# The price table of a kernel's own scheduler is replaced

## The chip, the cores and the metric

The kernel runs on one core of a Trainium2 chip. The metric is device time in microseconds (us) of one execution; the number quoted for a kernel is the median over its runs. The program is a whole two-block transformer step in fp32, and its inputs are read from HBM once per execution.

## The reference

A first block of two layers works on 512 latent tokens and 256 context tokens of width 1024. Each layer modulates its input (`w_ada`), projects it (`w_in`), runs four mixers of 256 columns each, gates the result, projects it out (`w_out`) and normalises:

```python
h = x * (1.0 + scale[:, None]) + shift[:, None]
...
o_f, _ = gla_chunk_scan(q, k_f, i, lf_f, s_cf)      # mixer a: gated linear attention, both directions
...
p = jax.nn.softmax(logits, axis=-1)                 # mixer b: dense attention with two key heads
...
w = p[:, :, 0] - lam * p[:, :, 1]                   # mixer c: differential attention
...
lw = jnp.where(allowed[None, :, None, None], lw, -jnp.inf)   # mixer d: window of 128 and all context
```

A second block of one layer works on the 512 latent tokens: a spatial gating unit, a sparse attention, two convolutions, gated branch projections, `w_out_2`, and an MLP of width 4096 with a squared ReLU.

## The kernel before

All big projections are done as three TensorE matmuls on rounded halves: a weight tile `raw` is loaded by a DMA, rounded to `whi` (fp32r), and the remainder goes to `wlo` (`split`, line 537); activations stand as such pairs too (`h`, `yh`/`yl`, `mix`, `hid`). `mm3` issues hi by hi, hi by lo, lo by hi. Everything else on TensorE is plain fp32 or fp32r: the scores of the attention mixers (`kc`, `kb` against `qs`), transposes against `ident`, and the products with V, which are written PV below (`vc`, `bdv`, `v` against the probabilities `p`).

What order the program's instructions stand in is set while the kernel is built, by a scheduler in the kernel itself. Every stage is a Python generator that yields the tiles it needs next. There are two kinds. **Fillers** are the weight stages, taken in a fixed sequence (`CFG["order"]`, line 2473; `choose`, line 679, lets the next one begin when SBUF has room for it). **Acts** are the stages of the mixers: attention units (`seg_c` line 1227 for mixer c, `seg_bd` line 1356 for b and d), the level chain of mixer a (`j_a`, line 1494), and small follow-ups. At most `wc`, `wb`, `wd` = 4 units of a segment run at a time, one more when no filler is left.

`turn` (line 649) picks what is emitted next. It holds an estimate of the time at which each engine is free and each tile is ready (`Est`, line 211). An act whose tiles are ready by the estimated PE time goes first; if none is, the filler goes; if that is not ready either, the estimated PE time jumps to the first that will be. `Est.op` (line 247) adds an instruction: it starts when its engine is free and its inputs are ready, and its output is ready `LAG` after its end. The prices of the instructions are in `K.time` (line 550). Two other decisions read the same estimates: `best` (line 481) sends a copy, a scaling or a subtraction that is marked `"*"` to the engine that would end it first, and `Psum.pick` (line 428) chooses the bank that is free first.

One unit of mixer c for a latent query tile does this: two score products per head pair into 768 columns of `banks`; on DVE a row maximum (`sm`); on ACT an exponential with a row sum (`p`); reciprocals; a scaling of one `p`; on DVE a `scalar_tensor_tensor` that combines the two; six transposes on PE; a copy back into `p`; and, once both heads of a tile are there, 12 PV matmuls of 128 columns (6 key tiles, 2 heads). Mixer a runs, per pair of heads, one product of `ks` and `qs` and then seven levels in a chain: a copy to `ks`, 12 matmuls of `qh` with `ks` in the first layer and 8 in the second (`level_mm`, line 1477), a masked copy into `att`, and updates of `qh` and `kh`.

At the start of the program the first `h` tiles are made by `co_first_h` (line 955): a scaled activation on ACT, then `split` into the pair.

The build runs twice with the same decisions: once to collect the lifetimes of the SBUF tiles, once to emit. All instructions pass through `Eng` (line 282 in the profile's rows).

Of the kernel before, what the change touches and what calls it, by code (L numbers as in the profile page):

```python
# [11 lines left out]
F32R = mybir.dt.float32r  # L12
# [6 lines left out]
D, S, CL = 1024, 512, 256  # L19
# [191 lines left out]
class Est:  # L211


    LAG = 90.0

    def __init__(self):
        self.t = dict(P=0.0, A=0.0, V=0.0, G=0.0, D=0.0)
# [29 lines left out]
    def op(self, eng, cost, outs, ins, lag=None):  # L247
        start = self.t[eng]
        for ap in ins:
            w, r, i = self.touch(ap)  # L250
            start = max(start, w[i].max())
        for ap in outs:
            w, r, i = self.touch(ap)
            start = max(start, w[i].max() - (self.LAG if eng != "D" else 0.0), r[i].max())
        end = start + cost
        self.t[eng] = end
        lag = self.LAG if lag is None else lag
        for ap in ins:
            w, r, i = self.touch(ap)
            r[i] = np.maximum(r[i], end)  # L260
        for ap in outs:
            w, r, i = self.touch(ap)
            w[i] = end + lag


class Eng:
# [5 lines left out]
    def __getattr__(self, op):  # L272
        f = getattr(self.real, op)

        def call(*a, **kw):
            aps = [x for x in a if hasattr(x, "ap") and hasattr(x, "tensor")]
            outs, ins = aps[:1], aps[1:]
            for n, x in kw.items():
                if hasattr(x, "ap") and hasattr(x, "tensor"):
                    (outs if n in ("accum_out", "out") else ins).append(x)  # L280
            self.k.time(self.eng, op, outs, ins, kw)
            return f(*a, **kw)  # L282
        return call
# [174 lines left out]
class K:  # L458
# [91 lines left out]
    def time(self, eng, op, outs, ins, kw):  # L550
        est = self.est
        if op == "dma_start":
            est.t["D"] = max(est.t["D"], est.t["P"])
            o = outs[0]
            n = int(np.prod(o.shape)) * 4
            est.op("D", 30.0 + n / 360.0, outs, ins, 2000.0)
            return
        if op in ("add_instruction",):
            return
        o = outs[0]  # L560
        n = int(np.prod(o.shape[1:]))
        if eng == "P":
            if op == "transpose":
                c = 107.0
            else:
                k = ins[0]
                m = int(np.prod(k.shape[1:]))
                if k.dtype == F32R:
                    c = max(107.0, n / 2.4)
                else:  # L570
                    c = max(107.0 if m > 64 else 67.0, n * (0.417 if m > 64 else 0.22 if m > 32 else 0.11)) * (2 if n < 512 and m > 64 else 4 if m > 64 else 2)
                    c = max(214.0, n * 1.67) if m > 64 else max(135.0, n * 0.89) if m > 32 else max(60.0, n * 0.42)
                    if k.shape[0] == 64:
                        c /= 2
            est.op("P", c, outs, ins)
            return
        for a in ins:
            n = max(n, int(np.prod(a.shape[1:])) if len(a.shape) > 1 else 1)
        if eng == "A":
            c = 60.0 + 0.95 * n + (90.0 if "accum_out" in kw else 0.0)  # L580
        elif eng == "V":
            ps = any(a.tensor.name == self.bank_name for a in outs + ins)
            fast = op in ("tensor_copy", "tensor_scalar", "memset") and not ps
            c = 70.0 + (0.6 if fast else 1.1) * n
        else:
            c = 90.0 + (2.0 if op == "tensor_tensor" else 1.0) * n
            if kw.get("op") == ALU.pow:
                c = 500.0 + 165.0 * n
        est.op(eng, c, outs, ins)

    @property
# [1934 lines left out]
```

## Time and profile before

| | |
|---|---|
| time, median of 3 runs | 1966.51 us (1965.34 to 1966.84) |
| profiled execution: time, span | 1970.03 us, 1968.3 us |
| granted TensorE clock, mean | 0.976 |
| PE busy | 1856.5 us, 94% |
| DVE, ACT, POOL busy | 1204.4, 622.7, 522.9 us |
| HBM read | 152.12 MB |

PE's busy time is the time in which at least one matmul is under way; what is left of the span is idle time, and a lowered clock makes busy time longer. In the trace the names of buffers stand without their numbers. A plain fp32 matmul that is no transpose stands in the trace as two records; an fp32r matmul or a transpose as one.

### The profile page before, as it was taken

What the parts mean: (1) busy time and instruction counts of PE and PEld (TensorE: products, weight loads), DVE (VectorE), ACT (ScalarE), POOL (GpSimd) and SP (SyncE); (2) the same over time, 40 slices, a digit from 0 to 9 for tenths busy, and PEclk for the clock granted to TensorE, in tenths of its full rate; (3) what the DMA queues carried; (4) which work ended last, traced back from release to release, by engine and by line L of the source; (5) the groups of instructions that cost most, each with busy time, mean ns of one, the idle gap of its engine ahead of it and who ended that gap; (6) DMA issues with size and microseconds to landing.
All of it is one profiled execution on the core that took longest, in us unless ns stands there. A gap on an engine that the chain in (4) does not pass through costs nothing.

```text
span 1968.3 us, 28571 instructions
## 1 busy us (share of the span) xinstructions
PE 1856.5 (94%) x11446; PEld 1539.2 (78%) x11446; DVE 1204.4 (61%) x2055; ACT 622.7 (32%) x1275; POOL 522.9 (27%) x453
## 2 busy tenths in 40 slices
PE   6899999899999999899998899999999999999999
PEld 4688667798877788786886787878788778888887
DVE  2648775655657747766566969764533665545542
ACT  2335444345520145444444321243423211000100
POOL 1314333532222324543233454411211220000000
PEclk9999989999999899999999999999999999999999
DMA  9100321100233301002124322121223222332121
GB/s 359 54 22 23 130 76 59 60 23 33 76 99 126 102 12 44 22 22 97 55 75 142 103 84 73 60 71 43 97 75 123 96 86 75 97 129 86 66 96 63
DMA packets 45380, 159.22 MB, mean 81 GB/s; under 512 B 5040, under 2 KB 5552, under 8 KB 44992
## 3 DMA queue, kind: packets, MB, share of 16 engines
q1 hardware_dynamic: 42224, 148.54, 21.9%
q10 hardware_dynamic: 3024, 8.85, 1.3%
q8 instruction: 90, 1.47, 0.3%
q14 instruction: 42, 0.34, 0.1%
HBM read 152.12 MB, written 5.26 MB: 80 GB/s over the span
## 4 chain that ended last, share of the span: by engine, by line
PE 42%; DVE 12%; POOL 4%; issue 3%; ACT 2%; DMA 1%; ACTq 0%; POOLq 0%; DVEq 0%; SPq 0%
PE banks L282 42%; DVE cacc L282 3%; POOL t L282 2%; DVE t L282 1%; DVE wlo L282 1%; DVE z L282 1%; DVE sm L282 1%; DVE h L282 1%; DVE p L282 1%; ACT p L282 1%; DVE xr L282 0%; DVE whi L282 0%; DVE gt L282 0%; POOL wlo L282 0%; DVE xn L282 0%
## 5 line engine op out<-in xcount | busy, mean ns | idle before, releaser
L282 PE MATMUL banks<-h,whi 128*128 128x512 f32 (+1 forms) x1968 | 584.0, 380 | 5.9 <-ACT h L282 2.8
L282 PEld LDWEIGHTS banks<-h,whi 128*128 128x128 f32 x1968 | 355.4, 192 | 68.2 <-ACT h L282 3.3
L282 PE MATMUL banks<-h,wlo 128*128 128x512 f32 (+1 forms) x984 | 368.6, 375 | 0.0
L282 PE MATMUL banks<-whi,h 128*128 128x256 f32 (+3 forms) x1344 | 337.5, 334 | 14.4 <-DVE h L282 7.9
L282 DVE TENSOR_TENSOR wlo<-raw,whi 128x1024 fp32r<-128x1024 f32 (+2 forms) x175 | 222.9, 1277 | 104.5 <-PE banks L282 59.7
L282 PEld LDWEIGHTS banks<-whi,h 128*128 128x128 f32 x1344 | 237.5, 195 | 40.4 <-DVE h L282 9.4
L282 PE MATMUL banks<-wlo,h 128*128 128x256 f32 (+3 forms) x672 | 221.8, 331 | 6.9 <-DVE wlo L282 5.6
L282 POOL TENSOR_TENSOR wlo<-raw,whi 128x1024 fp32r<-128x1024 f32 (+2 forms) x41 | 103.4, 2525 | 464.5 <-DMA out<-z 299.8
L282 PEld LDWEIGHTS banks<-h,wlo 128*128 128x128 f32 x984 | 188.0, 191 | 32.8 <-DVE wlo L282 0.4
L282 DVE TENSOR_REDUCE sm<-banks 128x1 f32<-128x768 f32 (+5 forms) x192 | 140.0, 750 | 59.7 <-PE banks L282 57.0
L282 ACT ACTIVATE p<-banks,sm 128x768 f32<-128x768 f32 (+5 forms) x192 | 141.3, 739 | 91.3 <-DVE sm L282 83.3
L282 ACT CAST whi<-raw 128x1024 fp32r<-128x1024 f32 (+2 forms) x88 | 88.3, 1006 | 224.0 <-PE banks L282 152.1
L282 PE MATMUL banks<-whi,hid 128*128 128x512 f32 x512 | 157.9, 389 | 0.0
L282 PEld LDWEIGHTS banks<-wlo,h 128*128 128x128 f32 x672 | 131.1, 195 | 18.1 <-DVE wlo L282 7.4
L282 DVE CAST whi<-raw 128x1024 fp32r<-128x1024 f32 (+2 forms) x104 | 74.9, 724 | 114.7 <-PE banks L282 97.1
L282 PEld LDWEIGHTS banks<-whi,hid 128*128 128x128 f32 x512 | 96.1, 188 | 20.0
L282 PE MATMUL banks<-ident,p 128*128 128x128 f32 x656 | 98.0, 282 | 10.2 <-DVE att L282 2.3
L282 ACT COPY p<-banks 128x768 f32<-128x768 f32 (+5 forms) x118 | 74.0, 633 | 92.9 <-PE banks L282 90.7
L282 PE MATMUL banks<-wlo,hid 128*128 128x512 f32 x256 | 99.6, 389 | 0.0
L282 POOL TENSOR_TENSOR t<-t,mhalf 128x1 f32<-128x1 f32 (+5 forms) x51 | 64.1, 1260 | 132.0 <-DVE t L282 128.4
L282 PEld LDWEIGHTS banks<-ident,p 128*128 128x128 f32 x656 | 75.4, 143 | 30.4 <-issue 7.6
L282 ACT ACTIVATE rl<-banks 128x512 f32<-128x512 f32 (+1 forms) x35 | 19.7, 562 | 169.2 <-PE banks L282 169.2
(334 smaller groups left out, 2963.3 us busy)
## 6 DMA issues: line engine op xcount, KB each, us to landing
raw<-wm SPq DMA_DIRECT2D x64, 512.0 KB, 3.5
raw<-win SPq DMA_DIRECT2D x60, 512.0 KB, 3.7
raw<-wada SPq DMA_DIRECT2D x48, 512.0 KB, 3.9
raw<-wgate SPq DMA_DIRECT2D x32, 512.0 KB, 3.5
raw<-wout SPq DMA_DIRECT2D x24, 512.0 KB, 3.5
raw<-w2f SPq DMA_DIRECT2D x10, 512.0 KB, 3.4
xr<-xtok SPq DMA_DIRECT2D x6, 512.0 KB, 4.6
x<-z SPq DMA_DIRECT2D x6, 512.0 KB, 2.6
```

What stands on the lines that cost most here:

```text
L282: return f(*a, **kw)
```

## The change

The prices in `K.time` and the readiness lags in `Est` are set to other numbers. No stage, tile, window or filler sequence is edited; the order of the instructions and the engines that `best` picks follow from the new numbers. In `Est.op`, `LAG` for DVE, ACT and POOL goes from 90 to 50 ns; PE's own lag, 90 before, is now 200. On PE the plain fp32 products get a price by the columns of the stationary operand (`m`) and its rows.

```diff
--- before.py
+++ after.py
@@ -211,7 +211,7 @@
 class Est:
 
 
-    LAG = 90.0
+    LAG = 50.0
 
     def __init__(self):
         self.t = dict(P=0.0, A=0.0, V=0.0, G=0.0, D=0.0)
@@ -251,7 +251,7 @@
             start = max(start, w[i].max())
         for ap in outs:
             w, r, i = self.touch(ap)
-            start = max(start, w[i].max() - (self.LAG if eng != "D" else 0.0), r[i].max())
+            start = max(start, w[i].max() - (0.0 if eng == "D" else 200.0 if eng == "P" else self.LAG), r[i].max())
         end = start + cost
         self.t[eng] = end
         lag = self.LAG if lag is None else lag
@@ -560,32 +560,32 @@
         o = outs[0]
         n = int(np.prod(o.shape[1:]))
         if eng == "P":
+            k = ins[0]
+            m = int(np.prod(k.shape[1:]))
             if op == "transpose":
-                c = 107.0
+                c = 110.0
+            elif k.dtype == F32R:
+                c = max(108.0, 0.4475 * n)
+            elif m > 64:
+                c = 0.42 * n if k.shape[0] == 64 else max(120.0, 1.74 * n)
+            elif m > 32:
+                c = 140.0 if k.shape[0] == 64 else max(54.0, 0.42 * n)
             else:
-                k = ins[0]
-                m = int(np.prod(k.shape[1:]))
-                if k.dtype == F32R:
-                    c = max(107.0, n / 2.4)
-                else:
-                    c = max(107.0 if m > 64 else 67.0, n * (0.417 if m > 64 else 0.22 if m > 32 else 0.11)) * (2 if n < 512 and m > 64 else 4 if m > 64 else 2)
-                    c = max(214.0, n * 1.67) if m > 64 else max(135.0, n * 0.89) if m > 32 else max(60.0, n * 0.42)
-                    if k.shape[0] == 64:
-                        c /= 2
-            est.op("P", c, outs, ins)
+                c = 0.213 * n
+            est.op("P", c, outs, ins, 200.0)
             return
         for a in ins:
             n = max(n, int(np.prod(a.shape[1:])) if len(a.shape) > 1 else 1)
         if eng == "A":
-            c = 60.0 + 0.95 * n + (90.0 if "accum_out" in kw else 0.0)
+            c = 170.0 + 0.93 * n + (100.0 if "accum_out" in kw else 0.0)
         elif eng == "V":
             ps = any(a.tensor.name == self.bank_name for a in outs + ins)
             fast = op in ("tensor_copy", "tensor_scalar", "memset") and not ps
-            c = 70.0 + (0.6 if fast else 1.1) * n
+            c = 110.0 + 0.58 * n if fast else 125.0 + 1.1 * n + (70.0 if op in ("scalar_tensor_tensor", "copy_predicated") else 0.0)
         else:
-            c = 90.0 + (2.0 if op == "tensor_tensor" else 1.0) * n
+            c = 200.0 + (2.3 if op == "tensor_tensor" else 1.05) * n
             if kw.get("op") == ALU.pow:
-                c = 500.0 + 165.0 * n
+                c = 700.0 + 165.0 * n
         est.op(eng, c, outs, ins)
 
     @property
```

**PE, mixer a's first pair of heads in the first layer.** `qh,ks` are the level matmuls, `kc,qs` scores of mixer c, `whi` and `wlo` with `h` the fillers. Before, levels 3 and 4 (`ks_2082`, `ks_2135`):

```order
L282 MATMUL banks<-qh_1805,ks_2082 128x128 x12
L282 MATMUL banks<-kc_1478,qs_1996 128x512
L282 MATMUL banks<-kc_1478,qs_1996 128x256
L282 MATMUL banks<-qh_1805,ks_2135 128x128 x3
L282 MATMUL banks<-kc_1478,qs_1996 128x512
L282 MATMUL banks<-kc_1478,qs_1996 128x256
L282 MATMUL banks<-qh_1805,ks_2135 128x128 x5
L282 MATMUL banks<-kc_1478,qs_1996 128x512
L282 MATMUL banks<-kc_1478,qs_1996 128x256
L282 MATMUL banks<-qh_1805,ks_2135 128x128 x4
L282 MATMUL banks<-ident_69,p_2028 128x128 x6
```

The same pair after, level 4 (`ks_2063`) and what follows it up to level 5:

```order
L282 MATMUL banks<-qh_1767,ks_2063 128x128 x12
L282 MATMUL banks<-kc_1557,qs_2024 128x512
L282 MATMUL banks<-kc_1557,qs_2024 128x256
L282 MATMUL banks<-kc_1557,qs_2024 128x512
L282 MATMUL banks<-kc_1557,qs_2024 128x256
L282 MATMUL banks<-ident_69,stg_2032 128x128 x4
L282 MATMUL banks<-whi_1608,h_95 128x256
L282 MATMUL banks<-wlo_1609,h_95 128x256
L282 MATMUL banks<-whi_1608,h_96 128x256
L282 MATMUL banks<-whi_1608,h_95 128x256
L282 MATMUL banks<-wlo_1609,h_95 128x256
L282 MATMUL banks<-whi_1608,h_96 128x256
```

And after, the start of that pair: the product with `qs`, levels 0 and 1.

```order
L282 MATMUL banks<-qs_1393,ks_1770 128x128 x12
L282 MATMUL banks<-kc_1557,qs_1733 128x512
L282 MATMUL banks<-kc_1557,qs_1733 128x256
L282 MATMUL banks<-qh_1767,ks_1820 128x128 x12
L282 MATMUL banks<-kc_1557,qs_1733 128x512
L282 MATMUL banks<-kc_1557,qs_1733 128x256
L282 MATMUL banks<-kc_1557,qs_1741 128x512
L282 MATMUL banks<-kc_1557,qs_1741 128x256
L282 MATMUL banks<-qh_1767,ks_1851 128x128 x2
L282 MATMUL banks<-kc_1557,qs_1741 128x512
L282 MATMUL banks<-kc_1557,qs_1741 128x256
L282 MATMUL banks<-qh_1767,ks_1851 128x128 x10
```

In the program before, levels 3 and 4 have only scores between them, and between the other levels of the pair stand fillers. In the new one, filler rows follow level 4, and the places with nothing but scores between level products are the two at the pair's start.

**PE, the end of the second layer's attention.** `kb,qs` and `dmask` are scores of mixer d, `ident,p` its transposes, `p,bdv` its PV matmuls, `yh`, `yl` with `whi`, `wlo` the output projection, which is the filler there. Before, the last scores and what follows:

```order
L282 MATMUL banks<-dmask_76,identr_74 128x128
L282 MATMUL banks<-kb_8746,qs_9405 128x256 x4
L282 MATMUL banks<-dmask_76,identr_74 128x128
L282 MATMUL banks<-kb_8746,qs_9405 128x256
L282 MATMUL banks<-whi_9425,yh_8919 128x512
L282 MATMUL banks<-ident_69,p_9358 128x128 x5
L282 MATMUL banks<-wlo_9426,yh_8919 128x512
L282 MATMUL banks<-whi_9425,yl_8920 128x512
L282 MATMUL banks<-whi_9425,yh_9011 128x512
L282 MATMUL banks<-wlo_9426,yh_9011 128x512
L282 MATMUL banks<-whi_9425,yl_9012 128x512
```

After, the last scores and what follows:

```order
L282 MATMUL banks<-kb_8746,qs_9494 128x256 x3
L282 MATMUL banks<-dmask_76,identr_74 128x128
L282 MATMUL banks<-kb_8746,qs_9494 128x256 x4
L282 MATMUL banks<-dmask_76,identr_74 128x128
L282 MATMUL banks<-kb_8746,qs_9494 128x256
L282 MATMUL banks<-ident_69,p_9467 128x128 x5
L282 MATMUL banks<-p_9467,bdv_7969 64x128
L282 MATMUL banks<-ident_69,p_9489 128x128 x5
L282 MATMUL banks<-whi_9155,yh_8834 128x512
L282 MATMUL banks<-ident_69,p_9509 128x128 x4
L282 MATMUL banks<-p_9489,bdv_7969 64x128
```

Before, 18 rows of the output projection stand between those scores and the transposes of the last units; the piece shows the first six of them and the transposes of an older unit. After, one projection row stands between the last scores and the transposes of the unit that they belong to (`p_9509`), beside transposes and a PV matmul of the two units ahead of it.

**DVE, the first `h` tiles.** `x_17` and `x_18` are columns of the input, `h_95` and `h_96` the pair for the latent tokens, `h_98` the remainder for the context tokens.

```order
 L282 CAST h_95<-x_17_99 128x512
 L282 TENSOR_TENSOR h_96<-x_17_99,h_95 128x512
+L282 CAST h_95<-x_18_101 128x512
 L282 TENSOR_TENSOR h_98<-x_17_99,h_97 128x256
 L282 TENSOR_TENSOR h_96<-x_18_101,h_95 128x512
-L282 TENSOR_TENSOR h_98<-x_18_101,h_97 128x256
 L282 TENSOR_TENSOR mod_103<-banks,vec_61 128x4
```

The rounding of every second `h` tile, which stood on ACT, is now on DVE ahead of the remainder of the tile before it, and one remainder has left DVE. The same swap follows in the next round and in the last. Over the whole program DVE has 166 subtractions into `wlo` where it had 175, and POOL 50 where it had 41; of the scalings of `p`, DVE has 30 (43 before), POOL 56 (41), ACT 66 (68). From a point near 1350 us of the old trace to the end, PE's rows are the same but for buffer numbers.

## Rows read from the trace of the kernel before

**Rows 1.** The page: the span.
```profile
span 1968.3 us, 28571 instructions
```

**Rows 2.** Stretches: length, then busy time of PE, PEld, DVE, ACT, POOL; PEclk; DMA share; GB/s.
```profile
114.00:565.00 451.00, 429.25 (x3511) 359.61 (x3510) 297.13 (x589) 216.41 (x478) 146.91 (x135) 0.97 0.18 59
710.00:1079.00 369.00, 343.52 (x2708) 288.04 (x2707) 251.16 (x426) 177.39 (x350) 139.74 (x131) 0.97 0.19 61
1079.00:1300.00 221.00, 199.03 (x1010) 174.42 (x1009) 187.63 (x312) 57.75 (x132) 103.42 (x83) 0.95 0.24 81
```

**Rows 3.** Whom PE waited for: us in total, times, longest us.
```profile
...
PE banks L282 <- DVE att L282: 7.6, 7, 2.4
PE banks L282 <- ACT p L282: 6.8, 14, 1.2
PE banks L282 <- POOL qh L282: 6.3, 3, 3.4
PE banks L282 <- POOL ks L282: 4.1, 3, 2.6
PE banks L282 <- DVE p L282: 3.5, 7, 1.8
PE banks L282 <- DVE qs L282: 3.5, 3, 2.5
PE banks L282 <- ACT qs L282: 2.7, 3, 1.3
```

**Rows 4.** Instructions by form: engine, operation, shapes xcount | busy us, mean ns | idle before.
```profile
L282 DVE TENSOR_REDUCE sm<-banks 128x1 f32<-128x768 f32 x96 | 88.6, 949 | 19.6 <-PE banks L282 17.8 <-ACT p L282 1.1
...
L282 ACT ACTIVATE p<-banks,sm 128x768 f32<-128x768 f32 x96 | 86.3, 904 | 57.3 <-DVE sm L282 49.6 <-POOL bd L282 2.7 <-PE banks L282 2.1
...
L282 ACT ACTIVATION_READ_ACCUMULATOR p<-banks,sm 128x1 f32 x192 | 38.1, 199 | 0.0
...
L282 DVE SCALAR_TENSOR_TENSOR p<-p,sm,p 128x768 f32<-128x768 f32 x32 | 36.8, 1153 | 6.5 <-ACT p L282 4.4 <-POOL p L282 1.9
```

**Rows 5.** PE's timeline from 330 and 386 us: start, us, engine, tile xcount.
```profile
330.70 1.55 PE L282 MATMUL banks<-p,bdv 128*64 128x128 f32 x24
332.18 0.98 PE L282 MATMUL banks<-ident,p 128*128 128x128 f32 x7
...
386.67 1.61 PE L282 MATMUL banks<-qh,ks 64*128 64x128 f32 x24
388.20 0.66 PE L282 MATMUL banks<-p,bdv 128*64 128x128 f32 x8
```

**Rows 6.** A stretch of MLP matmuls of 512 columns alone, columns as in rows 2.
```profile
1700.00:1750.00 50.00, 50.00 (x223) 41.39 (x222) 22.34 (x27) 1.65 (x2) 0.00 (x0) 1.00 0.28 95
```

**Rows 7.** Instructions by form, PE: records of the PV and level matmuls.
```profile
L282 PE MATMUL banks<-p,bdv 128*64 128x128 f32 x736 | 54.0, 283 | 0.3 <-DVE p L282 0.2
...
L282 PE MATMUL banks<-qh,ks 64*128 64x128 f32 x560 | 47.0, 301 | 10.4 <-POOL qh L282 6.3 <-ACT ks L282 1.5 <-DVE sm L282 1.2
...
L282 PE MATMUL banks<-p,vc 128*64 128x128 f32 x416 | 30.7, 278 | 0.2 <-DVE p L282 0.2
...
L282 PE MATMUL banks<-qs,ks 64*128 64x128 f32 x80 | 8.1, 346 | 3.7 <-POOL ks L282 3.7
```

**Rows 8.** The stretch 255 to 271 us, and a row of PE's timeline in it.
```profile
255.00:271.00 16.00, 12.40 (x93) 9.74 (x94) 13.96 (x21) 7.04 (x13) 7.39 (x7) 0.80 0.08 29
...
263.20 0.71 PE L282 MATMUL banks<-qh,ks 64*128 64x128 f32 x6 [2.00 <-POOL qh L282]
```

**Rows 9.** The end of the second layer's attention, columns as in rows 2.
```profile
1064.00:1079.00 15.00, 12.87 (x84) 9.63 (x85) 6.70 (x11) 6.74 (x11) 6.23 (x3) 1.00 0.29 96
```

**Rows 10.** Timelines of DVE and POOL near 35 us and of DVE near 66 us.
```profile
35.08 2.45 DVE L282 CAST h<-x 128x512 fp32r<-128x512 f32 x1 [0.29 <-ACT x L282]
...
34.88 2.37 POOL L282 TENSOR_TENSOR wlo<-raw,whi 128x1024 fp32r<-128x1024 f32 x1 [13.26 <-DMA raw<-wada]
...
65.85 0.43 DVE L282 CAST h<-x 128x512 fp32r<-128x512 f32 x1 [0.89 <-ACT x L282]
```

## Prediction

> **What bounds the kernel now.** I read the span first [rows 1], then the stretches [rows 2], then what ended PE's waits [rows 3]. TensorE carries the time. In the two attention stretches it is busy for 429.25 of 451 us and 343.52 of 369 us, so it idles 21.8 and 25.5 us, 47.3 together. The granted clock there is 0.97 in both: at most 0.03 x 820 = 24.6 us more go to stretches at the lower of its two levels (1.2 against 2.4 GHz), and these follow idle time, as the run at 255 us shows, with 3.6 us idle and a clock of 0.80 [rows 8]. So 71.9 us is all that a better order could take out of attention. In the stretch from 1079 to 1300 us DVE is busy 187.63 of 221 us and PE idles 22.0; that is DVE's work, and an order of stages does not shorten it. From about 1350 us on PE's rows are unchanged, and I price that part at nothing, since no wait there sees another producer in another place.
>
> The waits of attention are of two kinds [rows 3]. Those on the results of units (`p` from ACT 6.8 and DVE 3.5, `qs` from DVE 3.5 and ACT 2.7) are 16.5 us. Those on mixer a's level chain (`att` 7.6, `qh` 6.3, `ks` 4.1) are 18.0 us.
>
> **What the new prices say, against the rows.** Take the chain of a unit of mixer c: row maximum, exponential with row sum, combination. The rows have 949 + 904 + 199 + 1153 = 3205 ns [rows 4]. The old formulas give 915 + 880 + 915 = 2710, with three handoffs of 90 2980. The new ones give 970 + 984 + 1040 = 2994, with handoffs of 200, 50 and 50 3294. So the old table was short of the bare durations by 225 ns even with its handoffs, and the new one is 89 over. A matmul of 512 columns takes 50/223 = 224 ns [rows 6]; the price goes from 213 to 229. So far the table comes closer.
>
> It moves away at the small fp32 products. The 24 records of a PV run are 12 instructions by the code (6 key tiles, 2 heads), and they hold PE from 330.70 to 332.18, 123 ns each [rows 5]; the price goes from 135 to 54. A level of 12 instructions takes 386.67 to 388.20, 128 ns each [rows 5]; the price goes from 107 to 54. The new numbers are those of one record, and an instruction has two. With (736 + 416)/2 = 576 PV instructions and (560 + 80)/2 = 320 level instructions [rows 7] the scheduler's PE falls behind by 576 x 69 + 320 x 74 = 63 us over both layers. It then takes results for not ready that are, and emits filler in their place.
>
> **The change part by part.** *Waits on units.* With handoffs and DVE, ACT and POOL priced near the rows, a unit's next step is emitted later and more filler stands ahead of it. Bounds: nothing, where no filler is to be had, and all 16.5 us. I take two thirds, since the shortfall of 225 ns is gone in the table and some waits are of engines' queues that it still has wrong: 11.0 us, and the clock in proportion, 24.6 x 11.0/47.3 = 5.7. Together -16.7.
>
> *Waits on the level chain.* I cost this at nothing, with bounds of 9 us either way (half of 18.0). The order shows why: the levels that stood with only scores between them, where PE waited 2.00 us for `qh` [rows 8], are now followed by filler, but the pair starts with two places of the same kind. What is late next is `qh` again, one level earlier.
>
> *Ends of the layers.* At the end of the second layer the last scores had 18 projection matmuls of 0.224 us behind them, 4.0 us; now it is one. The last units need 3205 ns and more from scores to transposes [rows 4], and that cover is gone. The old end already idled 2.1 of 15 us [rows 9]. I take +3 per layer, since the first layer's last units stand among the projection's first rows in the same way: +6. Bounds: 0, if the filler spent earlier saved as much there, and +13, twice 42% of 16 us, which is what the bare run lost in idle time and clock (3.6 + 3.2 of 16) [rows 8].
>
> *Start.* Three roundings of `h` move from ACT to DVE, ahead of a remainder that PE waits for: 3 x 0.43 us [rows 10] = 1.3, bounds 0 and 2 x that, for ACT gets to its next activation sooner. I take +1.
>
> *Work moved to POOL.* Nine more remainders `wlo` are on POOL. While POOL ran such a one from 34.88 to 37.25, a DVE rounding that takes 0.43 us elsewhere took 2.45, and ended 0.28 us after it [rows 10]. Each can thus hold DVE up for 2.0 us: 18 us at most, nothing at least. DVE idles a third of both attention stretches, 1 - 548.29/820 [rows 2], and not every `wlo` meets such an operation, so I take +2. The 15 more scalings of `p` on POOL are priced near their length in the new table and have filler over them; should that be gone they are part of the ends above.
>
> The Trainium skill, page "SBUF — State Buffer", section "SBUF: two separate sides", says that DVE and GpSimd share a port pair under an exclusive lock, held for a whole instruction, against DVE operations in a two-port mode or with two SBUF inputs. The trace agrees in the one row cited; by that rule alone the sum would have up to +18 in this place where it has +2, and it speaks against moving work to POOL.
>
> **The sum.** -16.7 + 0 + 6 + 1 + 2 = -7.7 us. The profiled execution took 1970.0 us, 1.7 more than its span, and lies 3.5 above the median of the runs. 1970.0 - 7.7 - 3.5 = **1958.8 us**.
>
> **The rivals.** *Cover only moves (no change).* The scheduler has the same fillers and the same units; what one place gains another lacks. For it: the level chain's two bare places before and two after. Half of the gain on units then remains, -8.4 + 9 = +0.6: 1967.1 us. A run of this kernel tells a difference of about 0.2% (3.9 us) from none.
>
> *Filler spent too early (slower).* The 63 us by which the scheduler's PE lags behind are emitted as filler ahead of need, and the units late in each layer run bare, at 42% loss [rows 8]: 26.6 us in place of the 6 above. -16.7 + 26.6 + 3 = +12.9: 1979.4 us. It decides from (16.7 - 3)/0.42 = 33 us of filler on. For it: the tail of the second layer in the new order. Against it: level 4 of the first pair has filler behind it that it lacked.
>
> *POOL holds DVE.* Every added `wlo` blocks DVE for its length and PE waits for it: +18 in place of +2 gives +8.3, 1974.8 us. Against it: the waits on `wlo` are not among the long ones. [...]
>
> *The table does not do what it says*: this is so for the two fp32 prices, and lies in the second rival.
>
> **How the numbers follow.** 0.43 for the forecast, 0.21 for no change, 0.29 for filler spent early, 0.07 for POOL. So faster by over 0.2% 0.43, within it 0.21, slower 0.36. The order of some 8000 rows is new, and single waits of 1 to 3 us fall anew, which no row prices; that is why the chances lie close. Low end: the gain on units and clock twice as large, other terms +5, -28.4: 1938. High end: filler spent early, and POOL at +9 in place of +2: 1986.
>
> **What would show it.** Right: PE's waits on `p` and `qs` fall to some 6 us from 16.5, the clock of both attention stretches rises above 0.97, waits on `att`, `qh`, `ks` stay near 18, and the last 15 us before the second layer's projection idle some 5 us. Wrong: waits on `p` unchanged, or an attention stretch in which idle time gathers at its end; or DVE roundings and remainders that grow longer beside POOL. The forecast falls if the two attention stretches together, 820 us before, do not get shorter by some 10 us.

## The result, and the profile after

The changed kernel takes 1980.17 us, median of 4 runs (1979.28 to 1987.05); beside it the kernel before took 1966.03. The ratio is 1.0085, 95% interval 1.0062 to 1.0107: **slower** by 0.85%, where the forecast said 1958.8 and faster. The time lies in the stated range, and beside the second rival's 1979.4. The profiled execution has a span 9.3 us longer [rows 1], so the traces hold 9.3 of the 14.1 us between the medians.

The page of the changed kernel:

```profile
span 1977.6 us, 28679 instructions
...
PE 1853.5 (94%) x11446; PEld 1534.3 (78%) x11446; DVE 1178.9 (60%) x2040; ACT 625.0 (32%) x1279; POOL 545.4 (28%) x464
```

PE's busy time is 3.0 us shorter than before, so the loss is idle time. To find it, both traces have to be cut at the same work, not at the same microsecond: I cut each where PE had begun the same number of its 11,446 matmul records (449, 3958, 4578, 6867, 7285 and 8293). The second layer's attention is cut once more, ahead of its last 418 records. Stretches of the kernel before, columns as in [rows 2]:

```profile
710.00:1014.20 304.20, 283.90 (x2291) 241.16 (x2289) 210.11 (x346) 145.07 (x280) 117.20 (x115) 0.97 0.15 49
1014.20:1079.10 64.90, 59.73 (x419) 46.96 (x418) 41.15 (x81) 32.33 (x71) 22.54 (x16) 1.00 0.35 118
```

The changed kernel, first layer's attention, then the two pieces of the second's, then the stretch behind it:

```profile
112.50:576.10 463.60, 433.14 (x3510) 361.12 (x3510) 290.44 (x574) 218.67 (x482) 149.19 (x140) 0.98 0.18 60
...
717.80:1006.50 288.70, 276.51 (x2290) 236.14 (x2289) 203.45 (x348) 146.85 (x283) 120.80 (x110) 0.99 0.17 56
1006.50:1084.60 78.10, 63.54 (x419) 49.79 (x419) 43.41 (x82) 34.17 (x75) 26.83 (x19) 0.93 0.22 77
1084.60:1313.70 229.10, 203.15 (x1009) 177.38 (x1009) 177.50 (x312) 58.38 (x129) 92.97 (x75) 0.93 0.23 78
```

The first layer's attention took 451.1 us between the same records and now takes 463.6: 12.5 longer, with 30.5 us of PE idle where 21.8 were. The body of the second layer's is 15.5 shorter, idle 20.3 to 12.2, clock 0.97 to 0.99. Its end is 13.2 longer: idle 5.2 to 14.6, clock 1.00 to 0.93. The stretch behind it grew by 8.1, and what is left (start, first epilogue, the part from 1300 us) shrank by 9.0. The sum is 9.3.

Whom PE waited for, changed kernel (us, times, longest):

```profile
PE banks L282 <- ACT p L282: 16.3, 21, 3.3
...
PE banks L282 <- POOL wlo L282: 10.0, 9, 2.4
...
PE banks L282 <- ACT qs L282: 8.3, 5, 5.9
...
PE banks L282 <- DVE p L282: 4.1, 2, 2.4
...
PE banks L282 <- POOL ks L282: 2.8, 2, 2.0
PE banks L282 <- POOL qh L282: 2.7, 2, 1.5
...
PE banks L282 <- DVE att L282: 2.4, 5, 0.7
...
PE banks L282 <- DVE qs L282: 1.4, 2, 0.8
```

The waits on units, 16.5 us before [rows 3], are 16.3 + 4.1 + 8.3 + 1.4 = 30.1. Those on mixer a's chain, 18.0, are 7.9. On POOL's remainders `wlo` PE waits 10.0 us; the same row of the kernel before:

```profile
PE banks L282 <- POOL wlo L282: 2.7, 3, 1.3
```

By stretch, in us, from the same rows (`p` and `qs` of ACT and DVE; `att`, `qh` and `ks` of DVE and POOL):

| second number: changed kernel | units | level chain |
|---|---|---|
| first layer's attention | 6.0, 15.2 | 6.5, 6.9 |
| second layer's, body | 7.2, 6.6 | 11.5, 1.1 |
| second layer's, end | 2.2, 8.4 | 0, 0 |

So the gain in the body of the second layer is the chain's, which the forecast had at nothing, and hardly the units'. The rows of the body before:

```profile
PE banks L282 <- DVE att L282: 4.6, 3, 2.4
PE banks L282 <- POOL qh L282: 4.3, 2, 3.4
...
PE banks L282 <- POOL ks L282: 2.6, 1, 2.6
```

After, only this one is left of them there:

```profile
PE banks L282 <- DVE att L282: 1.1, 2, 0.6
```

A row "PE <- ACT `p`" is not always a wait for a result. The longest of the first layer stands before transposes that read no `p`:

```profile
218.61 1.51 PE L282 MATMUL banks<-ident,hq 128*128 128x128 f32 x6 [3.32 <-ACT p L282]
```

In the program the first of them writes columns of `banks` that the exponential it waits for still reads: PE waits for a bank, and which bank a stage gets is `Psum.pick`'s choice by the same estimates. Of the 16.3 us on ACT's `p`, 12.1 stand before matmuls that read no `p`, and the program's rows give this reason for each; in the kernel before, 5.0 of 6.8 stand before such matmuls.

The longest wait of all on units, 5.9 us on `qs` at the end of the second layer, shows a cause that the forecast did not have. The timeline of all engines there, changed kernel (start, us, engine, instruction, idle before and what ended it):

```profile
1042.92 0.59 ACT L282 COPY yo<-banks 128x512 f32<-128x512 f32 x1 [3.80 <-PE banks L282]
...
1043.51 1.05 POOL L282 TENSOR_SCALAR bc<-bc 128x1024 f32<-128x1024 f32 x1 [14.51 <-ACT yo L282]
...
1044.64 3.37 POOL L282 TENSOR_TENSOR xr<-xr,bc 128x1024 f32<-128x1024 f32 x1
1047.97 2.33 POOL L282 TENSOR_TENSOR wlo<-raw,whi 128x1024 fp32r<-128x1024 f32 x1
1048.04 3.34 DVE L282 TENSOR_TENSOR xr<-xr,bc 128x1024 f32<-128x1024 f32 x1 [2.23 <-POOL xr L282]
1050.34 0.37 ACT L282 CAST qs<-banks 128x256 fp32r<-128x256 f32 x1 [6.84 <-POOL wlo L282]
1050.77 1.01 PE L282 MATMUL banks<-kb,qs 128*128 128x256 f32 x3 [5.88 <-ACT qs L282]
...
1053.36 1.22 DVE L282 TENSOR_TENSOR xr<-xr,bc 128x1024 f32<-128x1024 f32 x1
```

ACT copies `qs` out of PSUM, and PE had written it 10 us earlier. It waited for POOL's remainder `wlo<-raw,whi`, with which `qs` has nothing to do. The program's rows say why:

```
732 L282 CAST qs_1048_9324<-banks_58 128x256 [waits Pool_49]
320 L282 TENSOR_TENSOR wlo_1041_9290<-raw_1030_9248,whi_1040_9289 128x1024 [waits DMAHW5_49,DVE_49]
```

`qs_1048` was given the SBUF place of `raw_1030`, and must not write there before the last reader of `raw_1030` is done. That reader stood on POOL behind a `bc` that had waited 14.51 us and an `xr` of 3.37. The profile puts the 14.51 down to ACT's `yo`, which `bc` does not read; by the program's rows it waits, beside earlier work on PE, DVE and ACT, for the DMA that brings it, issued at 1036.12.

Two pieces of that end, around this wait and behind the last scores:

```profile
1042.70:1056.00 13.30, 7.42 (x37) 6.59 (x36) 9.18 (x11) 4.25 (x10) 6.72 (x3) 0.74 0.03 11
...
1072.00:1081.20 9.20, 7.51 (x56) 5.30 (x56) 5.57 (x17) 4.82 (x13) 3.28 (x4) 1.00 0.27 100
```

The first has 5.9 us of idle and a clock of 0.74, worth some 1.9 us more by estimate (7.42 x 0.26): 7.8 of the 13.2. The second is the bare place that the forecast had read; it idles 1.7 us at the full clock.

Places are given out by the kernel itself (`Mem.place`, line 360), from the order of allocations and releases. A released place rests as long as the tiles in use and those at rest stay below a `share` of SBUF; it tries shares from 1.0 down until all fits. By the build's own count the kernel before holds at most 206,336 of 212,800 bytes per partition and is placed at share 0.82; the changed one holds 211,456 and gets 0.72.

### The profile page after: what moved, and what is told of

The parts are those of the page before. It is cut to its first block, busy times and chain, and to the rows that moved or that the text cites. A ratio compares the mean times of both kernels' runs of the same rounds, so it can differ in the third digit from the quotient of the medians.

```text
span 1977.6 us, 28679 instructions
## 1 busy us (share of the span) xinstructions
PE 1853.5 (94%) x11446; PEld 1534.3 (78%) x11446; DVE 1178.9 (60%) x2040; ACT 625.0 (32%) x1279; POOL 545.4 (28%) x464
## 3 DMA queue, kind: packets, MB, share of 16 engines
q1 hardware_dynamic: 42224, 148.54, 21.9%
## 4 chain that ended last, share of the span: by engine, by line
PE 71%; DVE 11%; POOL 6%; issue 4%; DMA 4%; ACT 3%; POOLq 0%; SPq 0%; DVEq 0%; ACTq 0%
PE banks L282 71%; DVE sm L282 2%; POOL t L282 2%; ACT p L282 2%; DVE wlo L282 1%; POOL wlo L282 1%; DVE t L282 1%; DMA x<-xT 1%; DMA raw<-wada 1%; DVE h L282 1%; DMA raw<-win 1%; DVE cacc L282 1%; ACT whi L282 1%; DVE z L282 0%; DVE whi L282 0%
## 5 line engine op out<-in xcount | busy, mean ns | idle before, releaser
L282 DVE TENSOR_TENSOR wlo<-raw,whi 128x1024 fp32r<-128x1024 f32 (+2 forms) x166 | 209.4, 1264 | 124.2 <-PE banks L282 58.7
L282 POOL TENSOR_TENSOR wlo<-raw,whi 128x1024 fp32r<-128x1024 f32 (+2 forms) x50 | 124.3, 2489 | 440.0 <-PE banks L282 324.2
L282 DVE CAST whi<-raw 128x1024 fp32r<-128x1024 f32 (+2 forms) x98 | 68.9, 708 | 102.3 <-DMA raw<-wm 62.8
L282 POOL TENSOR_SCALAR p<-p,sm 128x768 f32<-128x768 f32 (+4 forms) x56 | 51.6, 923 | 150.2 <-DVE sm L282 129.9
```

## The experiments

Three theories at the start. **A**: the second rival, fp32 prices per record make the scheduler's PE late, and filler is spent early. **B**: work moved to POOL holds up DVE. **C**: any small change of a price gives another order, and which wait falls where is chance. Ratios below are to the kernel before, with 95% intervals. One thing to know for all of them: the framework that builds the program may put an instruction ahead of others of its engine; in the kernel before about 4% of PE's rows no longer follow the row that the scheduler emitted ahead of them.

**e1: fp32 prices per instruction, otherwise the change.**

```diff
-                c = 0.42 * n if k.shape[0] == 64 else max(120.0, 1.74 * n)
+                c = 0.87 * n if k.shape[0] == 64 else max(120.0, 1.74 * n)
...
-                c = 140.0 if k.shape[0] == 64 else max(54.0, 0.42 * n)
+                c = 140.0 if k.shape[0] == 64 else max(54.0, 0.87 * n)
```

> The changed kernel with its two fp32 prices set per instruction in place of per record (PV and level matmuls of 128 columns 111 instead of 54). Theory A, filler spent early because these prices are too low: the loss at the ends of both layers goes, the gain in their middle stays, about 1960 us (1955 to 1967). Theory B, work moved to POOL collides with DVE (49 remainders wlo stay on POOL): no change, 1976 to 1984. Theory C, any table of about these numbers gives an order of its own, and which wait falls where is chance: anything from 1962 to 1985, and no ordering by the prices.

1965.78 us, 1.0001 (0.9985 to 1.0018): the loss is gone, as A said; C's bounds hold the time too. The build also gave this kernel another placement (share 0.80), so e1 alone does not tell order from places. The end of the second layer's attention in its trace:

```profile
1011.80:1079.10 67.30, 61.54 (x420) 48.86 (x418) 39.19 (x79) 33.09 (x73) 18.91 (x14) 0.95 0.34 105
```

67.3 us, where the change has 78.1 and the kernel before 64.9. B falls here as what the loss needs: 49 remainders are still on POOL.

**e2: the matmul prices of before, the rest of the change.** The `if eng == "P":` branch of the kernel before is put back; `est.op("P", c, outs, ins, 200.0)` stays.

> The changed kernel with all matmul prices of before, only the prices of ACT, DVE and POOL and the lags are new (46 wlo on POOL). Theory A: PV 135 and levels 107 are near or above their length, so no filler is spent early: about 1960 us (1955 to 1967). Theory B: 1974 to 1984. Theory C: anything from 1962 to 1985.

1994.39 us, 1.0141 (1.0118 to 1.0164). A missed by 27 us, and B's and C's bounds do not hold it either. The build's count is again 211,456 bytes, and the share found only 0.64.

**e3: only the matmul prices and PE's lag of the change, in the kernel before.**

> The kernel of before with only the matmul prices and PE's lag of the change (38 wlo on POOL, 41 before). Theory A: filler spent early without the gain on units: slower than the changed kernel, 1980 to 1995. Theory B: as before, 1962 to 1970. Theory C: anything from 1962 to 1985.

1974.77 us, 1.0044 (1.003 to 1.0059). Slower, but 5 us less than A's low end, and more than B said; C's bounds hold it.

**e4: the kernel before with another lag.**

```diff
-    LAG = 90.0
+    LAG = 92.0
```

> The kernel of before with its lag at 92 ns in place of 90, nothing else; more than half of PE's rows come to stand elsewhere. Theories A and B: as before within 3 us, 1963 to 1969. Theory C: off by 5 us or more to either side, though no price is nearer to or further from the trace.

1961.63 us, 0.9976 (0.9963 to 0.9989). Two nanoseconds of lag are worth 4 us, below A's and B's range and short of C's 5, so part of any such difference is chance.

With the shares beside the times (0.78 for e4, 0.82 for before, 0.80 for e1 and e3, 0.72 for the change, 0.64 for e2) a new theory, **D**: places given on too early make the kernel slow. It is tested by other placements with the same emission, engines and prices. For e5, e7 and e8 the placer starts at the share named, and a tile that found no place goes first in the next try; e6 starts the old placer at 0.64.

```diff
-        for share in np.arange(1.0, 0.5, -0.02):
+        for share in np.arange(0.82, 0.5, -0.02):
...
-            for long in (300, 100, 200, 500, 50):
-                at = self.fit(size, f0, rest, long)
+            self.first = []
+            for _ in range(160):
+                at = self.fit(size, f0, rest, 20)
...
+        order = self.first + [i for i in order if i not in self.first]
...
+                self.first = [i] + [j for j in self.first if j != i]
```

> The changed kernel, same emission by its scheduler, but its SBUF tiles are placed so that a freed place rests as long as in the kernel before (share 0.82; the change itself only found a placement at 0.72). Theory D, the new order keeps more tiles alive at once, freed places are handed out sooner, and instructions wait for the last reader of the tile that stood there: 1964 to 1971 us. Theories A (filler spent early) and B (POOL against DVE): unchanged, 1976 to 1984, since order and engines stay. Theory C, chance of single waits: 1970 to 1985.

1958.37 us, 0.9969 (0.9956 to 0.9981): 21.8 faster than the change, 6 below D's range, and faster than the kernel before. The same `qs_1048` in its program and its trace:

```
732 L282 CAST qs_1048_9324<-banks_58 128x256 [waits PE_49,Activation_49]
```

```profile
1038.10 0.37 ACT L282 CAST qs<-banks 128x256 fp32r<-128x256 f32 x1
1038.53 0.42 PEld L282 LDWEIGHTS banks<-kb,qs 128*128 128x128 f32 x3 [0.26 <-ACT qs L282]
```

With another place it no longer waits for POOL, and PE's 5.88 us became 0.26. A and B said no change here: neither is needed for the loss of the kernel as built. The same four stretches as above in this kernel:

```profile
115.70:570.60 454.90, 427.81 (x3511) 361.13 (x3510) 300.15 (x572) 216.02 (x478) 150.72 (x138) 0.98 0.18 60
711.10:1001.60 290.50, 280.28 (x2290) 238.49 (x2289) 205.28 (x343) 149.54 (x286) 114.00 (x109) 0.98 0.18 56
1001.60:1071.90 70.30, 62.56 (x419) 50.66 (x418) 36.79 (x77) 31.26 (x70) 20.14 (x18) 0.93 0.22 79
1071.90:1293.10 221.20, 200.53 (x1010) 174.76 (x1009) 184.02 (x316) 57.38 (x129) 97.12 (x77) 0.95 0.25 81
```

Against the change, 8.7 us went from the first layer, 7.8 from the second layer's end and 7.9 from the stretch behind it; the gain in the body stayed. The waits on units did not go back: they are 21.9 us, most of them in the row

```profile
PE banks L282 <- ACT p L282: 17.0, 20, 2.9
```

One limit: the emission is the same, but which rows pass others follows from the places. Counted in the two built programs, 313 of PE's 10,000 instructions and 936 of DVE's 2,040 have another successor. "Placement" in e5 to e8 means the places and this together.

> The kernel before, same emission by its scheduler, with its tiles placed at share 0.64 in place of 0.82, as the second experiment had. Theory D: 1980 to 1995 us. Theories A and B: unchanged, 1963 to 1969. Theory C: 1960 to 1975.

1980.12 us (1972.63 to 1981.61), 1.0069 (1.0042 to 1.0095): slower by 14, as D said, and outside the ranges of A, B and C.

> The second experiment's kernel (old matmul prices, new prices elsewhere; 1994 us at share 0.64) with its tiles placed at share 0.82. Theory D: 1965 to 1976 us. Theories A and B: unchanged, 1990 to 1997. Theory C: 1980 to 1997.

2006.28 us, 1.0209 (1.0185 to 1.0234): a miss for all theories, 12 slower where D had said some 24 faster.

> The kernel before with its tiles placed at share 0.90 in place of 0.82, same emission. Theory D: faster, 1955 to 1963 us, unless all places rest long enough already at 0.82. Theories A, B: unchanged, 1963 to 1969. Theory C: 1960 to 1972.

1985.33 us, 1.011 (1.0084 to 1.0136): a miss for all again, 19 slower. So the share is no measure of a placement. What stands is that placement, at the same emission, moved three kernels in four trials by -22, +14, +12 and +19 us: as much as the change did.

To separate order from places I held every instruction to the order of its emission and built that with two placements. In the second a place is given on once the former tile's last reader has ended by the scheduler's own estimate, with a margin where there is room; where nothing fits, the margin goes below zero and in the end is dropped.

```diff
-            return f(*a, **kw)
+            r = f(*a, **kw)
+            if r is not None and hasattr(r, "ins"):
+                self.k.tc.keep_in_program_order(r)
+            return r
```

```diff
+            live = np.where(d < i, f0[d] > i, f0[i] > d)
+            gap = np.where(d < i, a[i] - z[d], a[d] - z[i])
+            for m in tiers:
+                hit = d[live | (gap < m)]
```

Here `a` and `z` are a tile's first and last use by the estimate, and `tiers` are the margins, from 8 us down to -4 and to none. The prices under test feed this estimate too.

> The kernel before, with every instruction held to the order in which its scheduler emitted it (the framework that builds the program otherwise lets about 4% of PE's rows pass others); placement at share 0.82 as before. Nothing more is told by it alone; it is the base for the next three. Since a row whose place is not free yet can no longer be passed, 1975 to 2005 us.

> The changed kernel held to its emission order in the same way, placement at share 0.72 as the change has it. Theory D (waits for the former tenant of a place): slower than the kernel before held to its order by 15 us or more. Theory A (filler spent early, a matter of order alone): slower by 10 to 20 us.

> The kernel before held to its emission order, same rows on every engine as the run before last, but tiles placed by the scheduler's own estimated times: a place is given on only once the former tenant's last reader has ended by the estimate, with a margin of up to 8 us where there is room. Theory D: faster than the same order at share 0.82 by 10 to 30 us. Theories A and B: no change, since order and engines are the same.

> The changed kernel held to its emission order, tiles placed by estimated times in the same way. Theory D: faster than the same order at share 0.72 by 20 to 45 us, and within 8 us of the kernel before placed in that way, so that the price table itself is worth little either way. Theory A: 10 to 20 us slower than the kernel before placed in that way, since the order holds the loss.

| | old placement | placed by estimated times |
|---|---|---|
| kernel before | 2017.33 (e9) | 2015.81 (e11) |
| changed kernel | 2063.92 (e10) | 2035.42 (e12) |

All four are held to their emission; the two of a line have the same instructions in the same order on every engine. The old placement costs the changed order 28.5 us, in D's range, and the order before 1.5, where D had said 10 or more. The two orders stay 19.6 apart, as A said, where D had said 8 at most. On the old placement they are 46.6 apart, more than A's 10 to 20, and e9 itself lies 12 above its range. Of the second layer's attention, body and end of e11, then of e12:

```profile
721.90:1023.10 301.20, 280.10 (x2290) 238.16 (x2289) 213.54 (x347) 145.24 (x286) 119.70 (x117) 0.97 0.15 49
1023.10:1097.80 74.70, 62.58 (x420) 49.28 (x419) 55.65 (x93) 33.64 (x73) 25.76 (x17) 0.91 0.35 119
```

```profile
727.90:1031.20 303.30, 283.50 (x2291) 242.07 (x2291) 208.90 (x344) 145.48 (x283) 121.42 (x110) 0.95 0.14 46
1031.20:1122.60 91.40, 69.34 (x420) 53.36 (x419) 55.05 (x97) 35.90 (x80) 28.90 (x21) 0.84 0.29 106
```

The bodies differ by 2.1 us, the ends by 16.7: 12.1 us of idle against 22.1, clock 0.91 against 0.84. That is the second rival's place, but only in part its shape. PE's waits at e12's end are more on weight tiles than on units:

```profile
PE banks L287 <- ACT whi L287: 6.7, 2, 3.8
PE banks L287 <- ACT p L287: 5.2, 2, 4.8
PE banks L287 <- POOL wlo L287: 4.5, 3, 2.4
PE banks L287 <- POOL p L287: 2.5, 3, 1.5
```

Of the 10 us more idle than in e11, some 6 are on units (`p` and `qs` of all engines, 8.2 against 2.4). The longest of those, 4.8, goes back to DVE, where two `xr` products ahead of the unit's reciprocals took 6.55 us while POOL worked on remainders. The 3.8 on `whi` goes back to a DMA of `bc` that ACT waited for.

Which price makes the difference? **F** is the theory that the longer prices and lags of the other engines do. The next four are held and placed in the way of e11 and e12.

> The changed kernel with its fp32 prices per instruction, held to its emission order, tiles placed by estimated times. Base: 2016 us for the kernel before built in that way, 2035 for the changed one. Theory A (fp32 prices per record spend filler early): 2010 to 2020, with the loss at the end of the second layer gone. Theory F (longer prices and lags of DVE, ACT, POOL and PE move units back): 2030 to 2040. Theory C: anywhere from 2000 to 2045.

1992.77 us: 42.6 faster than e12, 23.0 faster than e11, and below the ranges of all three theories. Its body and end:

```profile
709.40:1002.10 292.70, 278.24 (x2291) 239.41 (x2290) 218.27 (x347) 144.20 (x280) 119.94 (x112) 0.98 0.14 46
1002.10:1082.50 80.40, 61.38 (x419) 48.66 (x418) 49.68 (x99) 35.79 (x79) 22.65 (x17) 0.94 0.33 114
```

In the profiles, 11.0 us of the gain on e12 come from the end, 10.6 from the body and 18.5 from what lies ahead of it.

> The changed kernel with the old matmul prices (new lags and new prices of the other engines), held and placed in the same way. Theory A: 2010 to 2020. Theory F: 2030 to 2045. Theory C: anywhere from 2000 to 2045.

2011.04 us: 24.4 faster than e12. A's range holds, and F's does not: the new prices of the other engines without the new matmul prices are not slower here than the kernel before. As built, the same prices were the slowest (e2, e7).

> The kernel before with only the new matmul prices and PE's lag, held and placed in the same way. Theory A: 2030 to 2045. Theory F: 2010 to 2025. Theory C: anywhere from 2000 to 2045.

2019.55 us, 3.7 over e11: a miss for A and in F's range. The new matmul prices, among the old prices of the other engines, cost next to nothing.

> The kernel before with lag 92 in place of 90, held and placed in the same way. Theories A and F: 2013 to 2019, as the kernel before. Theory C: off by 8 us or more, to either side.

2006.43 us, 9.4 under e11, as C said, and a miss for A and F: orders with prices 2 ns apart differ by this much. The 42.6 and 24.4 are above it, the 3.7 is not. But each table was built once, with a placement of its own, and e10 against e12 shows a placement to be worth 28.5 at one order; so 24.4 is not clear of chance, and 42.6 is one trial.

The last two change both, prices and placement, in the kernel as it is built, where rows may pass others:

> The changed kernel with its fp32 prices per instruction and its tiles placed at share 0.82, built as the change is (rows may pass others). If the two causes add, 1935 to 1950 us (1980 less 14 and less 22). If either alone takes back what there is, 1953 to 1963, as the changed prices with the better placement. If placements fall by chance, 1950 to 1980.

> The same prices, tiles placed by the scheduler's estimated times, rows may pass others. If the two causes add, 1935 to 1950 us. If either alone takes back what there is, 1953 to 1963. If placements fall by chance, 1950 to 1980.

1963.01 us, 0.9983 (0.9972 to 0.9995), and 1966.63 us, 1.0003 (0.9991 to 1.0016). They don't add. The first lies at the edge of "either alone", the second only in the range for chance. The fastest kernel of the study stays e5: the prices of the change as they are, with another placement.

## Why the prediction was wrong

The sum was -7.7 us; medians moved by +14.1, and the two attention stretches, which the forecast wanted some 10 us shorter, are 10.2 longer (820.2 to 830.4). Term by term:

- **Waits on units, -16.7 with the clock: failed.** The step was "I take two thirds, since the shortfall of 225 ns is gone in the table". The waits rose from 16.5 to 30.1 us: in the first layer from 6.0 to 15.2, at the end of the second from 2.2 to 8.4, and in its body they stayed (7.2 to 6.6). Two things were wrong in it. Three quarters of the largest row are waits for a bank and not for a unit's result; the forecast had read the whole row as results, and taken its two thirds of all of it. And I had taken a change of prices for a change of order alone. Order also decides which tiles are alive together, and so who stands on whose place; no term of the sum had that. With other places (e5) the waits are 21.9, still above 16.5: the step fails there too.
- **Level chain, 0: right in the first layer, wrong in the second.** 18.0 to 7.9 us, 1.1 beyond the bound of 9. In the first layer, whose order was read, it stayed (6.5 to 6.9); the fall is the second layer's (11.5 to 1.1), whose level order was not read. It is the one large gain of the change, and the forecast did not count on it.
- **Ends of the layers, +6 (0 to 13): the wrong place.** The second layer's end alone cost 13.2. Behind the last scores, where one projection row stands in place of 18, PE idles 1.7 us; some 7.8 go with the one wait for a place ahead of that, and e5's end is 7.8 shorter.
- **Start, +1: -1.6** (112.5 us to the same record, 114.1 before).
- **POOL, +2: 7.3**, but not in the way foreseen. PE waited for POOL's remainders themselves, 10.0 us against 2.7. DVE's own remainders did not grow, 1292 ns on average against 1304 before (before, then changed):

```profile
L282 DVE TENSOR_TENSOR wlo<-raw,whi 128x1024 fp32r<-128x1024 f32 x160 | 208.1, 1304 | 99.5 <-PE banks L282 59.7 <-ACT whi L282 27.2 <-POOL whi L282 4.6
```

```profile
L282 DVE TENSOR_TENSOR wlo<-raw,whi 128x1024 fp32r<-128x1024 f32 x151 | 194.6, 1292 | 115.5 <-PE banks L282 58.7 <-ACT whi L282 43.8 <-POOL whi L282 7.3
```

Single meetings are seen: the `xr` product at 1048.04, which reads two tiles in SBUF, took 3.34 us while POOL worked from 1047.97 to 1050.30, and 1.22 at 1053.36. That is what the Trainium skill, page "SBUF — State Buffer", section "SBUF: two separate sides", says of two-input DVE operations beside GpSimd; the trace agrees in that row. As what the loss needs it is out: e1 and e5 leave the work on POOL and lose nothing.

- **From 1079 us on, 0: wrong.** The stretch behind the second layer's attention grew by 8.1 us; with other places (e5) by 0.2. The part from 1300 us on, most of whose PE rows are the same, shrank by 4.3.

What the runs show as the cause of the loss is the placement that the new order drew: at the same emission other places, with the rows that pass others for them, take back 21.8 us (e5), more than the 14.1 lost, and the trace shows one such wait from the tile to PE. Why this table drew a bad one is not shown; the share does not tell.

The second rival had the sign and, at 1979.4, nearly the time; the time is luck. Its mechanism is not borne out: the idle time is not where units run bare late in a layer. The second layer's bare place idles 1.7 us, and of the first layer's 30.5 us of idle 25.3 lie ahead of its last 112:

```profile
112.50:464.00 351.50, 326.20 (x2639) 273.52 (x2637) 224.71 (x423) 167.76 (x360) 112.50 (x104) 0.98 0.17 56
```

With order held, taking back the fp32 prices goes with 42.6 us and all matmul prices with 24.4 (e13, e14), but only among the new prices of the other engines (e15), and as built the old matmul prices made it worse (e2). So that these prices cost time through filler spent early is argued, not shown. It is luck, too, that e5's 1958.37 meets the forecast's 1958.8: its waits on units are up and its chain is down.

What stays open: what the new order is worth apart from its places. Every run has one placement, four trials of other places moved the time by 12 to 22 us, and no rule tried here foretells a good one.

## What to carry to other kernels

A scheduler's price table can come nearer to the trace in most entries and the kernel still be slower. An entry read per trace record must be multiplied by the records of an instruction, even though these runs do not settle what that mistake cost. Where a kernel places its own buffers, a new order is also a new placement, so judge a change of order only after other placements of the same order, here worth -22 to +19 us. When the profile says that an engine waits for one that produces nothing the waiter reads, look in the program's rows before giving it a cause: of the three such waits here one was for a place in SBUF (`qs`), one for a bank of PSUM (`hq`), and one for a DMA (`bc`).

## What was not expected of the hardware and the build

Holding all instructions to the order of emission cost 54 us in the kernel before (2017.33 against 1963.60 beside it) and 84 in the changed one (2063.92 against 1980.17): in this kernel the rows that pass others are worth more than any difference between price tables seen here. And a run-to-run spread of 10 us in one program (1960.75 to 1970.93 over 22 runs of the kernel before) is as large as most of the effects; only the medians of several runs tell these apart.
